# Down projection of a feed-forward: PSUM products copied by ScalarE and added to x by accumulating DMAs

## The chip, the cores and the metric

One core of one Trainium2 chip runs the program. The metric is the device time of one execution in microseconds (us); lower is better. A measurement of this kernel tells a change from none at about 2%.

## What is computed

Two sequences of 512 and 256 tokens, 1024 features wide, go through the same two-layer trunk in float32. Each layer is a half-weighted feed-forward, a mixer (layer 0: an S5 recurrence beside neighbourhood attention; layer 1: windowed attention), and a second half-weighted feed-forward. A norm ends the trunk.

```python
def swiglu(x, wg, wu, wd):
    return (jax.nn.silu(x @ wg) * (x @ wu)) @ wd        # wg, wu: 1024 x 2816, wd: 2816 x 1024
...
        x = x + 0.5 * swiglu(rms_norm(x, norm_ffn[layer, 0]), w_ffn_gate[layer, 0],
                             w_ffn_up[layer, 0], w_ffn_down[layer, 0])
```

The change concerns the last product of `swiglu`, the one with `wd`, and its addition to `x`.

## The kernel before

**Tiles.** The 768 tokens are six tiles of 128 tokens; `x` stays in SBUF as six tiles of 128 x 1024 float32, `x0` to `x5`, always visited in the order 4, 5, 0, 1, 2, 3. The program runs six stages one after the other: feed-forward 0, the mixer of the even layer, feed-forwards 1 and 2, the mixer of the odd layer, feed-forward 3.

**Arithmetic.** A float32 operand is used as two float32r parts, a rounded one and the rest: `split` (L88, L89) has ScalarE (ACT) write the rounded part and VectorE (DVE) the difference. Every product then takes three matmuls. Weights come through SyncE's DMA queue (SP) into `raw` tiles (seven buffers of 512 KB), are summed by DVE where the fast product needs it (L124 to L134), and are split into `whl` tiles (eight buffers). `take` keeps up to four split tiles ready ahead of the product that uses them.

**A feed-forward.** The 2816 features are 22 blocks, taken in 11 pairs, 0 to 10. For a pair, the gate and the up product (`quad`) are done by a Strassen-Winograd form with seven products of 12 matmuls each (L247): in order p1, p6, p5, p7, p2, p3, p4 from pair 2 on. They share PSUM banks: p1 is copied by ACT (L261); p6 goes to a second bank, from which DVE makes `u2` with that copy (L273); p5 to a third, copied by ACT (L279); p7 is then accumulated on top of p6's bank, so TensorE (PE) can start p7 only when L273 has read it. ACT applies silu (L314), DVE multiplies (L317), and the pair's activations are split into `hl`.

**The down projection.** `rows` has six steps, one for each token tile. A step makes two halves of 512 output features; a half is six matmuls into one of eight PSUM banks (L362). Then DVE computes `x = 0.5 * o + x` on that half straight from PSUM (L365). The steps of pair b-1 stand between the gate and the up product of pair b (`middle` in `ffn`). The steps of the last pair, 10, stand at the end with `tail` given: there, `before` and `after` start the next stage's norm on each tile.

**Order.** Within an engine instructions run in a fixed order, which a scheduler sets when the program is built; the order on PE and SP follows the source closely. GpSimd (POOL) has nothing to do in feed-forwards 1 to 3 but one small norm operation per tile. In feed-forward 0 it builds the matrices of S5 (`s5_matrices`), whose steps are spread between the steps of the pairs from pair 2 on (`next(extra, None)`). For each of 16 pairs of S5 groups, POOL computes two matrices (`start`, L579 to L595; the DMA W2d of L600 is queued in the middle of it), PE transposes one of them and makes small products (`finish`, L605 to L616), ACT copies the result, and POOL sends it out (`store`, DMAs W1d and Ed, L623 and L624). The next `start` reuses the space that W1d reads.

Of the kernel before, what the change touches and what calls it, by code (L numbers as in the profile page):

```python
# [37 lines left out]
# neighbourhood attention: (first query, queries, first key, keys) in the order (column, row)  # L38
NA_Q = [(0, 128, 0, 256), (128, 128, 64, 256), (256, 128, 192, 256), (384, 128, 256, 256),
        (512, 128, 512, 160), (640, 128, 608, 160)]  # L40
# key blocks (first key, keys) of the windows above
# [5 lines left out]
class Trunk:  # L47
# [20 lines left out]
    def warm(self, after):  # L68
        """have the table of the square root loaded as soon as the column "after" is there"""
        w = self.cp.tile([P, 1], F32, tag="warm", name="warm", bufs=2)  # L70
        self.nc.scalar.activation(w, after, AF.Sqrt, bias=self.one, scale=0.0)
# [13 lines left out]
    def split(self, hl, lo, src):  # L85
        """hl (rounded) + lo = src, exactly"""
        nc = self.nc
        nc.scalar.copy(hl, src)  # L88
        nc.vector.tensor_sub(lo, src, hl.bitcast(F32))  # L89

# [6 lines left out]
    def weights(self):  # L97
        """the weights of the whole trunk"""
# [15 lines left out]
        def quad(n, q, b, r1=None):  # L114
            """the parts and sums of two blocks of features; without the head if r1, the first, is given"""
            k = lambda z: (n, q, b, z)
            headed, r1 = r1 is not None, self.raw(self.a[n][q, 2 * b]) if r1 is None else r1
            a11, a12 = r1[:, :512], r1[:, 512:]
            if not headed:
                yield k("11"), self.part(a11)  # L120
            r2 = self.raw(self.a[n][q, 2 * b + 1])
            a21, a22 = r2[:, :512], r2[:, 512:]
            s1 = self.wp.tile([P, 512], F32, tag="st", name="st", bufs=2)
            v.tensor_add(s1, a21, a22)  # L124
            v.tensor_sub(a21, a11, a21)
            v.tensor_sub(a11, s1, a11)
            yield k("s2"), self.part(a11)
            yield k("s1"), self.part(s1)
            if b < 2:
                yield k("22"), self.part(a22)  # L130
            yield k("s3"), self.part(a21)
            if not headed:
                yield k("12"), self.part(a12)
            v.tensor_sub(a12, a12, a11)  # L134
            yield k("s4"), self.part(a12)
            if b > 1:
                yield k("22"), self.part(a22)
# [57 lines left out]
    def norm_half(self, t, out):  # L195
        """sum of squares of the first half of token tile t"""
        ss = self.cp.tile([P, 4], F32, tag="ss", name="ss", bufs=6)
        self.nc.scalar.activation(out[:, 0:512], self.x[t][:, 0:512], AF.Square, accum_out=ss[:, 0:1])  # L198
        self.nc.gpsimd.tensor_scalar(ss[:, 1:2], ss[:, 0:1], 1.0 / DM, EPS, ALU.mult, ALU.add)  # L199
        return ss  # L200

    def norm_rows(self, t, gb, out, ss, parts=1):
        """out = rms_norm of token tile t"""
        nc = self.nc
        nc.scalar.activation(out[:, 512:1024], self.x[t][:, 512:1024], AF.Square, accum_out=ss[:, 2:3])
        nc.scalar.activation(ss[:, 3:4], ss[:, 2:3], AF.Sqrt, bias=ss[:, 1:2], scale=1.0 / DM)
        nc.vector.reciprocal(ss[:, 0:1], ss[:, 3:4])
        for e in range(parts):
            c = slice(e * DM // parts, (e + 1) * DM // parts)
            nc.vector.scalar_tensor_tensor(out[:, c], self.x[t][:, c], ss[:, 0:1], gb[:, c], ALU.mult, ALU.mult)  # L210
# [7 lines left out]
    def gemm(self, o, w, act, k0, n, kk=range(KM), last=KM - 1):  # L218
        """o[128 features, n tokens] = w^T act, w stationary; w and act hold four blocks of 128 features to a tile"""
        for k in kk:  # L220
            for j, i in ((0, 0), (0, 1), (1, 0)):
                self.nc.tensor.matmul(o, w[k // 4][:, j, k % 4 * P : (k % 4 + 1) * P], act[i][k // 4][:, k % 4, k0 : k0 + n],  # L222
                                      start=k == 0 and (j, i) == (0, 0), stop=k == last and (j, i) == (1, 0))

    def ffn(self, q, norm, tail, extra=None):
        """gate and up by Winograd's form of Strassen's product over 2 blocks of features, of inputs and of tokens"""
# [4 lines left out]
        with ExitStack() as ctx:  # L231
# [18 lines left out]
            def quad(n, b, use):  # L250
                """steps of the four blocks; use(feature block, token half, value)"""
# [85 lines left out]
            for b in range(1, NF // 2):  # L337
                g, u = (z[2:] for z in (g1, u1)) if b == 1 else pair(b)
                middle = self.rows(hs, q, b - 1, pos)
                if b == NF // 2 - 1:  # L340
                    middle.insert(0, lambda: self.warm(at(1, 0)[:, 0:1]))
                for s in (*g, *middle, *u):
                    s()
                    if b > 1:
                        next(extra, None)
            for s in self.rows(hs, q, NF // 2 - 1, pos, tail):
                s()

    def rows(self, hs, q, b, pos, tail=None):
        """steps of x += 0.5 h wd over a pair of blocks of features"""  # L350
# [3 lines left out]
        def step(t):  # L354
# [3 lines left out]
            for half in range(2):  # L358
# [5 lines left out]
                xs = self.x[t][:, half * 512 : (half + 1) * 512]  # L364
                nc.vector.scalar_tensor_tensor(xs, o, 0.5, xs, ALU.mult, ALU.add)  # L365
                if tail and half == 0:
                    st["t"].before(t)
            if tail:
                st["t"].after(t)

        return [lambda t=t: step(t) for t in TILES]

    def out_pass(self, name, kb, half, act, tail=None):
        """steps of x[:, half] += act w over k-block kb (4 of 128 features); act(part, k) has all tokens"""
# [24 lines left out]
    def fgemm(self, f, hn, evac, norm=None, kk=KM):  # L399
        """steps of a feature block of act @ w, feature-major; f names the weights, evac(psum, first token, tokens)"""  # L400
# [17 lines left out]
    def s5_matrices(self, pool, spare):  # L418
# [10 lines left out]
        class Room:  # L429
            """carves blocks out of tiles"""  # L430
# [26 lines left out]
        def exp(out, x):  # L457
            """exp to float32's accuracy"""
# [51 lines left out]
        # (a - 1) / lambda  # L510
# [15 lines left out]
        # powers 0..8  # L526
# [40 lines left out]
        def start(q):  # L567
            """a pair of groups: W2 (state -> outputs), W1 (inputs -> state)"""
# [28 lines left out]
        def finish(q):  # L597
            """W1 transposed, E (inputs -> outputs)"""
# [44 lines left out]
    def mixer0(self, norm, tail):  # L643
# [4 lines left out]
        with ExitStack() as ctx:  # L648
            mp = ctx.enter_context(self.tc.tile_pool(name="mix0", bufs=1))

            # inputs of S5, in (chunk position, channel) rows
# [14 lines left out]
            def qkv(h):  # L666
                """steps of a head pair's values, queries and keys, in the order (column, row)"""
# [28 lines left out]
            def na(h):  # L696
                """steps of a head pair; q is overwritten by the output, feature-major"""
# [65 lines left out]
            # chunk inputs of the states; both directions run from slot to slot, the reversed one backwards in time  # L763
# [31 lines left out]
            # outputs of S5: chunk inputs through M, states before the chunk through W2  # L795
# [54 lines left out]
            # the neighbourhood half of the output projection around the gate of S5  # L850
# [25 lines left out]
    def mixer1(self, norm, tail):  # L876
        nc, a = self.nc, self.a
        hn = norm.hn
        with ExitStack() as ctx:
# [4 lines left out]
            # a key head's two parts above each other, the first part in the rows that its queries have  # L884
# [11 lines left out]
            # (query tile, first key tile, key tiles, first column of the bias)  # L896
# [20 lines left out]
            def att(m, store):  # L917
                """steps of the heads of key heads 2m and 2m+1"""
                bias, pend, pts, qq = [] if m else [bias0], {}, [], {}

                def queries(t):
                    """the first parts twice above each other, and the second parts"""
# [146 lines left out]
def weave(main, *sides):  # L1069
    """emit the steps of main with those of the sides spread between them"""  # L1070
    done = [0] * len(sides)
    for i, m in enumerate(main):
        m()
        for k, s in enumerate(sides):
            while done[k] < round((i + 1) * len(s) / len(main)):
                s[done[k]]()
                done[k] += 1
# [6 lines left out]
class NormOut:  # L1084
    """final rms_norm, a token tile at a time"""
# [17 lines left out]
class NormT:  # L1103
    """rms_norm, transposed to feature-major in two parts, a token tile at a time"""
# [41 lines left out]
class NormS(NormT):  # L1146
    """the same as the sums that ffn multiplies with; tokens of tiles 4, 5, 0 and of 1, 2, 3 face each other"""
# [46 lines left out]
    def rest(self):  # L1194
        """the parts that later products take, a step for each"""
# [39 lines left out]
def _na_index(t):  # L1235
    """row of the padded table for each (query, key) of query tile t"""
# [9 lines left out]
def _layout(i):  # L1246
# [13 lines left out]
    # heads of the odd layer: tile (m, r) holds head r of key heads 2m and 2m+1  # L1260
# [5 lines left out]
    # S5  # L1266
# [11 lines left out]
    # biases by constant index; the last entry of the padded table is the masked one  # L1278
# [26 lines left out]
```

## Time and profile before

| | us |
|---|---|
| median of 2 runs (2750.31 and 2751.83) | 2751.07 |
| span of the profiled execution | 2751.6 |
| PE busy in it | 2695.9 (98%) |
| DVE busy | 2008.4 (73%) |
| ACT busy | 1176.3 (43%) |
| POOL busy | 340.6 (12%) |
| share of PE in the chain that ended last | 92% |

The span is the time from the first to the last instruction of one profiled execution; the page gives no other time for that execution, and its span lies between the two runs. An engine's idle time costs only where another engine, in the end PE, waits for it. In the tables of stretches and in timelines, PEld is the loading of PE's weights, which runs beside its matmuls.

### The profile page before, as it was taken

Reading aid. Unit: us, or ns where it says so; the run is one execution under the profiler, and the core shown is the slowest. Engines: PE = TensorE matmul, PEld = TensorE weight load, DVE = VectorE, ACT = ScalarE, POOL = GpSimd, SP = SyncE. Lnnn points to the kernel's source line nnn. Section 1 sums busy time; section 2 is a strip of 40 time slices with the busy share of each in tenths; the row PEclk is TensorE's granted clock in tenths of the full one; section 3 lists DMA queues with packets and bytes.
Section 4 is the critical chain, followed back from the end, with each engine's and each line's share of the span. In section 5 each row is a group of like instructions: output and inputs, shape, how many; then the busy total and the mean of one; then the engine's idle time right before and its main releaser. Section 6 shows DMA issues by size and latency. Waiting matters only on the chain.

```text
span 2751.6 us, 38966 instructions
## 1 busy us (share of the span) xinstructions
PE 2695.9 (98%) x14636; PEld 2422.3 (88%) x14636; DVE 2008.4 (73%) x3878; ACT 1176.3 (43%) x2464; POOL 340.6 (12%) x688
## 2 busy tenths in 40 slices
PE   7999999998999999999999999999999999999998
PEld 7988988888888999999989999999876689999997
DVE  8967776772964887677789776767557678777776
ACT  6333333343565633333354333334457664333333
POOL 0156654300840000000000000000000000000000
PEclk9999999999999999999999999999999999999999
DMA  4122222316244222121203121211201123122221
GB/s 155 65 90 85 90 90 77 127 54 134 89 125 142 81 81 85 54 85 54 88 29 122 62 77 62 79 61 39 100 16 39 45 72 108 63 76 68 71 70 54
DMA packets 81245, 217.48 MB, mean 79 GB/s; under 512 B 22848, under 2 KB 29632, under 8 KB 80800
## 3 DMA queue, kind: packets, MB, share of 16 engines
q1 hardware_dynamic: 77152, 203.91, 23.4%
q0 software_dynamic: 3904, 11.08, 1.2%
q8 instruction: 115, 1.88, 0.3%
q14 instruction: 74, 0.61, 0.1%
HBM read 199.17 MB, written 17.89 MB: 79 GB/s over the span
## 4 chain that ended last, share of the span: by engine, by line
PE 92%; DVE 3%; DMA 2%; ACT 2%; POOL 1%; issue 1%; SPq 0%; DVEq 0%; ACTq 0%; POOLq 0%
PE ps L247 44%; PE ps L362 25%; PE ps L222 8%; PE ps L389 5%; PE ps L957 1%; PE ps L990 1%; PE ps L956 1%; PE ps L978 1%; PE ps L1133 1%; PE ps L1009 1%; PE ps L774 1%; PE ps L616 1%; DVE raw L210 1%; PE ps L746 1%; DVE whl L89 0%
## 5 line engine op out<-in xcount | busy, mean ns | idle before, releaser
L88 ACT CAST whl<-raw 128x512 fp32r<-128x512 f32 x796 | 480.3, 621 | 943.7 <-PE ps L362 446.6
L247 PE MATMUL ps<-bt,whl 128*128 128x384 f32 x4224 | 764.6, 336 | 8.9 <-DVE ct L273 8.9
L247 PEld LDWEIGHTS ps<-bt,whl 128*128 128x128 f32 x4224 | 737.9, 189 | 12.5 <-DVE ct L273 10.1
L362 PE MATMUL ps<-whl,hl 128*128 128x512 f32 x3168 | 732.7, 391 | 0.0
L89 DVE TENSOR_TENSOR whl<-raw,whl 128x512 fp32r<-128x512 f32 x796 | 550.6, 705 | 220.2 <-ACT whl L88 209.2
L362 PEld LDWEIGHTS ps<-whl,hl 128*128 128x128 f32 x3168 | 593.9, 188 | 123.5 <-ACT hl L88 0.9
L247 PE MATMUL ps<-b,whl 128*128 128x384 f32 x3168 | 580.3, 336 | 0.0
L247 PEld LDWEIGHTS ps<-b,whl 128*128 128x128 f32 x3168 | 555.1, 189 | 3.5 <-ACT hct L617 0.3
L365 DVE SCALAR_TENSOR_TENSOR x<-ps,x 128x512 f32<-128x512 f32 x528 | 361.5, 689 | 217.5 <-PE ps L362 215.3
L199 POOL TENSOR_SCALAR ss<-ss 128x1 f32<-128x1 f32 x42 | 11.3, 270 | 1787.2 <-ACT raw L198 1787.2
L222 PE MATMUL ps<-hn,whl 128*128 128x256 f32 (+1 forms) x1248 | 231.2, 342 | 1.4 <-ACT hn L88 1.4
L222 PEld LDWEIGHTS ps<-hn,whl 128*128 128x128 f32 x1248 | 191.8, 190 | 31.8 <-issue 3.3
L88 ACT CAST hl<-hct 128x384 fp32r<-128x384 f32 x176 | 86.9, 512 | 50.8 <-DVE hct L317 44.9
L389 PE MATMUL ps<-whl,ob 128*128 128x512 f32 x432 | 105.2, 399 | 0.0
L89 DVE TENSOR_TENSOR hl<-hct,hl 128x384 fp32r<-128x384 f32 x176 | 98.3, 577 | 7.7 <-ACT hl L88 7.4
L389 PEld LDWEIGHTS ps<-whl,ob 128*128 128x128 f32 x432 | 80.7, 190 | 19.7 <-issue 2.2
L279 ACT COPY ct<-ps 128x384 f32<-128x384 f32 x88 | 42.3, 481 | 102.4 <-PE ps L247 102.4
L314 ACT ACTIVATE hct<-ct 128x384 f32<-128x384 f32 x88 | 46.3, 526 | 91.3 <-DVE ct L285 79.9
L284 DVE TENSOR_TENSOR ct<-ps,hct 128x384 f32<-128x384 f32 x88 | 48.9, 556 | 29.3 <-PE ps L247 29.1
L124 DVE TENSOR_TENSOR st<-raw 128x512 f32<-128x512 f32 x88 | 62.6, 712 | 10.1 <-DMA raw<-in_w_gate 9.2
L958 DVE CUSTOM_DVE_ANT_0 raw<-ps,gb,sk 128x256 f32<-128x256 f32 (+1 forms) x96 | 48.6, 525 | 29.0 <-PE ps L957 25.8
L392 DVE TENSOR_TENSOR x<-ps,x 128x512 f32<-128x512 f32 x48 | 33.0, 688 | 48.6 <-PE ps L389 48.6
(235 smaller groups left out, 2632.8 us busy)
## 6 DMA issues: line engine op xcount, KB each, us to landing
raw<-in_w_gate SPq DMA_DIRECT2D x92, 512.0 KB, 3.6
raw<-in_w_up SPq DMA_DIRECT2D x92, 512.0 KB, 3.6
raw<-in_w_down SPq DMA_DIRECT2D x88, 512.0 KB, 3.7
raw<-in_w_in_even SPq DMA_DIRECT2D x16, 512.0 KB, 3.6
raw<-in_w_in_odd SPq DMA_DIRECT2D x10, 512.0 KB, 4.8
W2d<-raw POOLq DMA_DIRECT2D x16, 256.0 KB, 2.4
W1d<-hct POOLq DMA_DIRECT2D x16, 256.0 KB, 3.0
raw<-W1d SPq DMA_DIRECT2D x8, 512.0 KB, 5.5
```

The lines of the kernel that those rows point to most:

```text
L88: nc.scalar.copy(hl, src)
L89: nc.vector.tensor_sub(lo, src, hl.bitcast(F32))
L124: v.tensor_add(s1, a21, a22)
L222: self.nc.tensor.matmul(o, w[k // 4][:, j, k % 4 * P : (k % 4 + 1) * P], act[i][k // 4][:, k % 4, k0 : k0 + n], start=k == 0 and (j, i) == ...
L247: nc.tensor.matmul(o, w[:, j, k * P : (k + 1) * P], B[z][:, i, k], start=first and k == 0 and (j, i) == (0, 0), stop=k == 3 and (j, i) == ...
L279: nc.scalar.copy(bank["r5"], bank[3])
L284: v.tensor_add(u3, bank[2], bank["p1"])
L314: nc.scalar.activation(at(f, t), o, AF.Silu)
L362: nc.tensor.matmul(o, h[i][:, pos[t] * P : (pos[t] + 1) * P], w[half][:, j], start=n == 0 and (j, i) == (0, 0), stop=n == len(hs) - 1 and ...
L365: nc.vector.scalar_tensor_tensor(xs, o, 0.5, xs, ALU.mult, ALU.add)
L389: nc.tensor.matmul(o, act(i, k)[:, t * P : (t + 1) * P], st["w"][k][:, j], start=m == 0, stop=m == 11)
L958: nc.vector.tensor_tensor_reduce(p[:, e, :n], s[:, :n], bias[0][:, par * 4 + h, c0 : c0 + n], -1.0, sk[:, 1, hh + h : hh + h + 1], ALU.add ...
```

## The change

In all pairs but the last of a feed-forward, ACT multiplies the PSUM half by 0.5 into one half of a tile `y` (128 x 1024, three buffers), and after both halves POOL issues a DMA that adds the whole `y` tile to `x[t]` in SBUF. In the last pair, where `tail` is given, DVE's instruction stays. The program is also built with `dynamic_dma_scratch_size=4096`. Comments that the new file drops are left out here.

```diff
-                middle = self.rows(hs, q, b - 1, pos)
+                middle = self.rows(fp, hs, q, b - 1, pos)
...
-            for s in self.rows(hs, q, NF // 2 - 1, pos, tail):
+            for s in self.rows(fp, hs, q, NF // 2 - 1, pos, tail):
...
-    def rows(self, hs, q, b, pos, tail=None):
+    def rows(self, pool, hs, q, b, pos, tail=None):
...
-                xs = self.x[t][:, half * 512 : (half + 1) * 512]
-                nc.vector.scalar_tensor_tensor(xs, o, 0.5, xs, ALU.mult, ALU.add)
-                if tail and half == 0:
-                    st["t"].before(t)
+                if tail:
+                    xs = self.x[t][:, half * 512 : (half + 1) * 512]
+                    nc.vector.scalar_tensor_tensor(xs, o, 0.5, xs, ALU.mult, ALU.add)
+                    if half == 0:
+                        st["t"].before(t)
+                else:
+                    if half == 0:
+                        st["y"] = pool.tile([P, DM], F32, tag="y", name="y", bufs=3)
+                    nc.scalar.activation(st["y"][:, half * 512 : (half + 1) * 512], o, AF.Copy, scale=0.5)
             if tail:
                 st["t"].after(t)
+            else:
+                nc.gpsimd.dma_start(self.x[t], st["y"], accum_op=ALU.add)
...
-    nc = _bacc.Bacc("TRN2", target_bir_lowering=False, num_devices=1)
+    nc = _bacc.Bacc("TRN2", target_bir_lowering=False, num_devices=1, dynamic_dma_scratch_size=4096)
```

The order of instructions on PE and SP is the same before and after. Source lines above 349 have other numbers after: the new copy is L372, the accumulating DMA L376, and each line of `s5_matrices` is seven higher (L600 becomes L607, L623 becomes L630).

On ACT, in feed-forward 1 around the down projection of a pair, before: silu (L314), the casts of weights that follow it, and the copy of the up product's p1 (L261).

```order
L314 ACTIVATE hct<-ct 128x384
L88 CAST whl<-raw 128x512
L314 ACTIVATE hct<-hct 128x384
L88 CAST whl<-raw 128x512 x4
L261 COPY hct<-ps 128x384
L88 CAST whl<-raw 128x512
```

The same place after:

```order
L314 ACTIVATE hct<-hct 128x384
L372 ACTIVATE y<-ps 128x512 x10
L88 CAST whl<-raw 128x512
L372 ACTIVATE y<-ps 128x512
L88 CAST whl<-raw 128x512
L372 ACTIVATE y<-ps 128x512
L88 CAST whl<-raw 128x512 x2
L261 COPY hct<-ps 128x384
```

The twelve copies into `y` now stand between the last silu and the four casts, the last two of them among the casts; L261 stands behind all of them.

On POOL, in feed-forward 0 around the down projection of pair 3, before: the end of an S5 `start` and the `store` that follows.

```order
L600 DMA W2d<-raw 128x512
L592 TENSOR_TENSOR raw<-hct 128x2x128
L593 TENSOR_TENSOR hct<-s5k,raw 128x256
L594 TENSOR_TENSOR hct<-s5k,raw 128x256
L595 TENSOR_TENSOR raw<-hct 128x2x128
L623 DMA W1d<-hct 128x512
```

The same place after (x_81 and x_82 are token tiles 4 and 5, x_77 to x_80 tiles 0 to 3):

```order
L607 DMA W2d<-raw 128x512
L599 TENSOR_TENSOR raw<-hct 128x2x128
L600 TENSOR_TENSOR hct<-s5k,raw 128x256
L601 TENSOR_TENSOR hct<-s5k,raw 128x256
L602 TENSOR_TENSOR raw<-hct 128x2x128
L376 DMA x_81<-y 128x1024
L376 DMA x_82<-y 128x1024
L376 DMA x_77<-y 128x1024
L376 DMA x_78<-y 128x1024
L376 DMA x_79<-y 128x1024
L376 DMA x_80<-y 128x1024
L630 DMA W1d<-hct 128x512
```

All six accumulating DMAs of the pair stand behind the whole S5 `start`, and the `store` stands behind all six.

## Rows read from the trace of the kernel before

**Rows 1.** Stretches by stage: length, busy us (instructions) by engine, clock, DMA share, GB/s

```profile
core 0: us, PE busy (x) PEld busy (x) DVE busy (x) ACT busy (x) POOL busy (x), PEclk, DMA share, GB/s
25.00:600.00 575.00, 558.88 (x3116) 510.41 (x3116) 438.50 (x776) 210.75 (x427) 230.48 (x370) 0.98 0.26 86
926.00:1425.00 499.00, 499.00 (x2647) 468.06 (x2646) 387.55 (x649) 197.01 (x381) 0.91 (x4) 1.00 0.23 73
1433.00:1935.00 502.00, 502.00 (x2666) 470.52 (x2664) 389.90 (x653) 196.44 (x380) 1.76 (x4) 1.00 0.23 74
2241.00:2738.00 497.00, 497.00 (x2633) 466.15 (x2632) 383.85 (x643) 191.28 (x366) 0.84 (x3) 1.00 0.23 73
```

**Rows 2.** Chain that ended last, in feed-forward 1: start us, length us, what

```profile
1123.62 29.14 PE ps L247 x168
1152.77 16.36 PE ps L362 x72
```

**Rows 3.** Timeline, one down projection: start us, us, engine, instruction, [idle before <-releaser]

```profile
1152.61 16.52 PE L362 MATMUL ps<-whl,hl 128*128 128x512 f32 x72
...
1155.57 0.69 DVE L365 SCALAR_TENSOR_TENSOR x<-ps,x 128x512 f32<-128x512 f32 x1 [0.68 <-PE ps L362]
...
1167.12 0.62 ACT L88 CAST whl<-raw 128x512 fp32r<-128x512 f32 x1 [13.14 <-PE ps L362]
...
1171.07 6.40 PE L247 MATMUL ps<-bt,whl 128*128 128x384 f32 x36
...
1171.35 0.47 ACT L261 COPY hct<-ps 128x384 f32<-128x384 f32 x1
...
1173.42 0.56 DVE L273 TENSOR_TENSOR ct<-ps,hct 128x384 f32<-128x384 f32 x1 [0.36 <-PE ps L247]
```

**Rows 4.** Groups by line and shape: xcount | busy us, mean ns | idle before, releasers

```profile
L365 DVE SCALAR_TENSOR_TENSOR x<-ps,x 128x512 f32<-128x512 f32 x528 | 361.5, 689 | 217.5 <-PE ps L362 215.3
...
L124 DVE TENSOR_TENSOR st<-raw 128x512 f32<-128x512 f32 x88 | 62.6, 712 | 10.1 <-DMA raw<-in_w_gate 9.2 <-DMA raw<-in_w_up 0.9
...
L981 ACT COPY pt<-ps 128x512 f32<-128x512 f32 x56 | 30.1, 590 | 24.2 <-PE ps L978 23.9
...
L600 POOL DMA_DIRECT2D W2d<-raw x16 | 10.2, 634 | 0.0
```

**Rows 5.** DMA issues: count, KB each, median us from issue to landing

```profile
raw<-in_w_gate SPq DMA_DIRECT2D x92, 512.0 KB, 3.6
...
gb<-in_gqa_bias SPq DMA_DIRECT2D x2, 1536.0 KB, 6.8
```

**Rows 6.** Two stretches of feed-forward 1, columns as in rows 1

```profile
1123.62:1152.77 29.15, 29.15 (x170) 29.15 (x169) 24.23 (x42) 14.13 (x27) 0.00 (x0) 1.00 0.36 109
1152.77:1169.13 16.36, 16.36 (x73) 13.51 (x73) 9.52 (x15) 1.77 (x3) 0.00 (x0) 1.00 0.00 1
```

**Rows 7.** Waits of PE in 25 to 600 us: us in total, times, longest

```profile
PE ps L247 <- DVE ct L273: 8.9, 3, 4.0
...
PE ps L605 <- POOL raw L595: 5.7, 2, 2.9
```

**Rows 8.** Timeline of POOL and PE in feed-forward 0, columns as in rows 3

```profile
131.24 0.62 POOL L585 TENSOR_TENSOR hct<-s5k,raw 128x256 f32<-128x256 f32 x1
...
140.33 1.06 POOL L594 TENSOR_TENSOR hct<-s5k,raw 128x256 f32<-128x256 f32 x1
141.44 2.35 PE L247 MATMUL ps<-bt,whl 128*128 128x384 f32 x12 [1.93 <-DVE ct L273]
...
234.62 16.52 PE L362 MATMUL ps<-whl,hl 128*128 128x512 f32 x72
...
242.57 0.74 POOL L595 TENSOR_TENSOR raw<-hct 128x256 f32<-128x256 f32 x1
...
253.09 0.60 PE L605 MATMUL ps<-ident,raw 128*128 128x128 f32 x4
...
255.58 2.70 PE L247 MATMUL ps<-bt,whl 128*128 128x384 f32 x14
```

## The prediction

> **What bounds the kernel now.** I read the table of stretches first. In feed-forwards 1, 2 and 3 PE is busy for the whole of 499, 502 and 497 us, at a granted clock of 1.00, the 2.4 GHz level [rows 1]. The chain of waits says the same from the other side: in the steady part it consists of nothing but PE's products, 29.14 us of gate and up and 16.36 us of down projection for each pair, 45.5 us in all [rows 2]. DVE is the next engine, 388 of 499 us, and ACT has 197. So a busy DVE is not a waited-for DVE there. The one feed-forward in which PE idles is the first, 575.0 - 558.9 = 16.1 us [rows 1]. The waits of PE in it name DVE (8.9 us in three stops) and POOL (5.7 us in two) [rows 7]. That is all that a lighter DVE could give back in the stages that the change touches, about 0.5% of the run, before any cost.
>
> **What the change removes and adds.** Four stages x 10 pairs x 12 halves = 480 DVE instructions of 0.689 us go, 331 us of DVE. ACT gets 480 copies of 128x512 from PSUM; the nearest row is its copy of that shape, 0.590 us [rows 4], 283 us in all. POOL gets 240 accumulating DMAs of 512 KB. The PE order is unchanged, so in feed-forwards 1 to 3 removing DVE work gives 0: PE waits for nothing there.
>
> **ACT's copies** fall into a hole. Write R for the start of a down projection (1152.77). PE makes a half every 16.36 / 12 = 1.363 us. ACT idles for 13.14 us of that time, waiting for PE to free a weight buffer, until 1167.12 = R + 14.35 [rows 3]. Ten copies fit in front of that cast, one per half: the tenth half ends at R + 13.63, its copy at about R + 14.3. The other two stand among the casts. Price: 0, hidden by PE's own 16.36 us. Without that cover they would cost at most 12 x 0.59 = 7.1 us a pair.
>
> **The ring of three y tiles** is the wait that is added. DVE starts on the second half at 1155.57, R + 2.8 [rows 3]; ACT's copy in its place is done at R + 3.4, where the first DMA is issued, and the next two follow at R + 6.1 and R + 8.9. Tiles four, five and six reuse those buffers, and their first copies are due at R + 9.6, R + 12.3 and R + 15.0. Behind a waiting copy on ACT stand the casts and L261; DVE's L273 waits for L261, and PE's product p7 for L273. From the sixth tile's first copy to the end of L273 lie two copies (1.18), three casts (1.86), L261 (0.47) and L273 (0.56), with hand-overs 4.2 us. PE comes to p7 after three products, two of them in the 6.40 us row of three [rows 3]: R + 16.36 + 6.2 = R + 22.6. So PE stops only if the third DMA lands after R + 18.4.
>
> No accumulating DMA stands in this trace, so its time is an estimate. A load of 512 KB lands 3.6 us after its issue and one of 1536 KB after 6.8 [rows 5]: 2.0 us fixed and 1.6 us per 512 KB. Lower bound of the data time: one pass, 1.6 us. Upper: four passes, 6.4 us. I take two passes, y and x both read and the write beside them, 3.2 us, as the nearest to what must be moved. The DMA engines are idle in this stretch (share 0.00, against 0.36 in the products) [rows 6], so three transfers queue only behind one another: they land at R + 8.6, 11.8 and 15.0, each no later than its copy is due. Price 0. With data time s the third lands at R + 5.4 + 3s, which reaches R + 18.4 at s = 4.33 us. This is the figure from which the forecast tips. The smaller descriptor scratch could make an issue wait for an earlier DMA to land. At most three of these are in flight; I put 0, and as the other end one landing of 5.2 us, of which R + 18.4 - R - 15.0 = 3.4 us is slack: 1.8 us a pair.
>
> Here the Trainium skill (Collectives: The Full Stack, The bandwidth ceiling: the fold count and why AG ≠ RS ≠ AR) says that an add in the DMA path costs no cycles of its own but needs two source reads on one read ring, and so halves the rate of a copy. By it the data time would also be 3.2 us, worked out from the copy's row; no run here shows it yet.
>
> What else the transfers touch: the last three of a pair run into the products, beside weight loads at 109 GB/s [rows 6]. DVE's first use of a weight load waited for a DMA only 10.1 us in the whole run over 88 instructions [rows 4], so loads come early, and I price their delay at 0 (bounds 0 to 1.6 us a pair, one transfer). The last pair adds to x by DVE and needs pair 9's DMAs, which have the up product of pair 10 (14.6 us, half of 29.14) to land: 0.
>
> **Feed-forward 0, POOL.** Here POOL's order matters. In pair 3, W2d's group ends at 242.57 + 0.74 = 243.3, and all six DMAs stand behind it; the first y is ready at 234.8 + 3.4 = 238.2 [rows 8]. Issued back to back from 243.3, the third DMA lands at 243.3 + 2.0 + 9.6 = 254.9. PE stops after 234.8 + 18.4 = 253.2, or 255.7 since the small S5 products from 253.09 to 255.58 stand in front of p6 [rows 8]: between 0 and 1.7 us. In five more pairs some S5 instructions stand in front of a DMA, or the reverse. I take 2 us for all six, between 0 and 10. An issue itself takes POOL 0.63 us [rows 4], 60 x 0.63 = 38 us beside 230 of 575 busy: hidden.
>
> **Feed-forward 0, DVE.** The stop of 1.93 us at 141.44 comes while POOL works on its first S5 `start` beside DVE's sums [rows 8]. DVE's set-up for that start shares the two first down projections with 24 removed instructions, 16.5 us, so it should end some 10 us earlier and the start with it: I take 1.9 us back (bounds 0 and 1.9). The two other DVE stops come in the products, where nothing is removed but the last two halves: 0.
>
> The skill (SBUF — State Buffer, SBUF: two separate sides) adds that VectorE and GpSimd lock each other out of a shared port when a VectorE operation reads two SBUF tensors. L365 reads only one, so its removal would free no port. The trace agrees: POOL's sums take 0.62 us beside L365s and 1.06 us beside two-input sums [rows 8]. By that rule the later stops stay, which lowers the chance of the first rival below.
>
> **Sum.** 2751.6 (span) - 1.9 + 2 = 2751.7; the span lies 0.5 above the median of the runs. I predict 2751.
>
> **Rivals.**
> 1. The lighter DVE clears all stops of feed-forward 0: 2751 - 8.9 - 5.7 = 2736. For it: PE's waits name DVE. Against: two of the three stops lie in stretches that lose no DVE work.
> 2. POOL's single queue is the new wait, in feed-forward 0 alone: an S5 `start` held behind a DMA that waits for its y makes PE wait at L605, as it does twice already. At the upper price of 10 us: 2761, at twice that 2771.
> 3. The accumulating DMA is slow, and the ring of three holds ACT up: slower than before. It decides from s = 4.33 us. With both reads and the write in turn, s = 4.8, the third lands at R + 19.8, PE stops 1.4 us a pair, 40 pairs: 56 us, 2807. At four passes, s = 6.4: 6.2 us a pair, 2999. For it: no row shows this operation, and the slack is 3.4 us over three transfers. Against: the DMA engines are idle when it starts.
>
> That the change does not do what it says I leave without a chance: the built order shows copies and DMAs where the diff puts them.
>
> **How the numbers follow.** Forecast 0.60, rival 1 0.08, rival 2 0.15, rival 3 0.17. The forecast's own range is 2745 to 2757, from the bounds of its small terms. The whole range goes from 2738, near rival 1, to 2810, which takes in rival 3 up to three passes and leaves out its upper part. About 2% (55 us) is what a measurement tells from no change. Faster by more would need a PE that does less: 0.01. Slower by more is rival 3 from three passes on: 0.14. Within: 0.85.
>
> **What would show it.** Right: PE without idle time in feed-forwards 1 to 3; the accumulating DMA about 5 us from issue to landing; ACT near 1460 us busy, DVE near 1680; no wait of a y copy on a DMA above 1 us. Wrong: PE waits at L247 named L273, or ACT waits of L372 on the DMA, repeated at each pair (rival 3); PE waits at the transposes of S5 grown beyond 6 us (rival 2); a landing later than 6.2 us after the issue in feed-forwards 1 to 3 (R + 9.6 less R + 3.4) would make the ring step false.

## The result, and the profile after

The changed kernel takes 2774.49 us (2771.62 to 2777.36) against 2751.07: ratio 1.0082, interval 1.0062 to 1.0102. Run again later, in one batch with other variants, it took 2765.62 us, ratio 1.0062 (1.0040 to 1.0083). So it is 0.6 to 0.8% slower, where no change was predicted. That is less than the 2% at which a single measurement tells a change from none; both intervals lie wholly above 1. The time lies in the whole range that was given, 2738 to 2810, and above the forecast's own range of 2745 to 2757.

Stretches of the kernel after, columns as in [rows 1]; the rows are feed-forwards 0, 1, 2 and 3:

```profile
24.00:623.00 599.00, 572.25 (x3174) 521.54 (x3172) 375.19 (x670) 285.17 (x564) 285.58 (x431) 0.97 0.54 137
946.00:1447.00 501.00, 501.00 (x2658) 469.80 (x2657) 310.71 (x533) 268.61 (x505) 52.68 (x64) 1.00 0.56 136
1454.00:1951.00 497.00, 497.00 (x2634) 466.00 (x2633) 305.48 (x524) 263.37 (x492) 52.45 (x63) 1.00 0.56 136
2265.00:2770.00 505.00, 502.92 (x2656) 470.54 (x2655) 311.58 (x536) 265.70 (x503) 53.34 (x66) 1.00 0.56 137
```

Feed-forwards 1 and 2 are as full of PE work as before (the 2.1 idle us of the last row lie in its last 5 us, at the end of the stage). DVE gave up some 80 us in each, ACT took some 70, and the share of the DMA engines went from 0.23 to 0.56. The chain of waits there is the same as in [rows 2]:

```profile
1144.18 29.14 PE ps L247 x168
1173.32 16.36 PE ps L362 x72
```

The loss is in feed-forward 0, where 599.0 - 572.3 = 26.8 us are idle against 16.1 [rows 1]. To find the place I set the starts of the down projections beside each other. Timeline of PE in feed-forward 0, kernel before:

```profile
274.42 0.60 PE L605 MATMUL ps<-ident,raw 128*128 128x128 f32 x4
...
285.35 13.81 PE L362 MATMUL ps<-whl,hl 128*128 128x512 f32 x60
...
501.65 16.52 PE L362 MATMUL ps<-whl,hl 128*128 128x512 f32 x72
...
549.77 16.52 PE L362 MATMUL ps<-whl,hl 128*128 128x512 f32 x72
```

The same view of the kernel after, with the stops between them in brackets:

```profile
229.75 16.52 PE L362 MATMUL ps<-whl,hl 128*128 128x512 f32 x72
...
274.13 0.33 PE L612 MATMUL ps<-ident,raw 128*128 128x128 f32 x1 [3.83 <-POOL raw L599]
276.20 0.90 PE L612 MATMUL ps<-ident,raw 128*128 128x128 f32 x3 [1.74 <-POOL raw L602]
...
280.34 4.21 PE L247 MATMUL ps<-bt,whl 128*128 128x384 f32 x12
...
291.15 13.80 PE L362 MATMUL ps<-whl,hl 128*128 128x512 f32 x60
...
375.24 0.55 PE L612 MATMUL ps<-ident,raw 128*128 128x128 f32 x3 [1.19 <-POOL raw L602]
...
509.39 16.52 PE L362 MATMUL ps<-whl,hl 128*128 128x512 f32 x72
...
536.18 2.35 PE L247 MATMUL ps<-bt,whl 128*128 128x384 f32 x12 [1.38 <-DVE ct L273]
...
545.96 4.21 PE L247 MATMUL ps<-bt,whl 128*128 128x384 f32 x12 [3.27 <-DVE ct L284]
...
565.37 16.52 PE L362 MATMUL ps<-whl,hl 128*128 128x512 f32 x72
```

| from the start of | before, us | after, us | difference |
|---|---|---|---|
| the span to pair 3's down projection | 234.62 | 229.75 | -4.9 |
| pair 3's to pair 4's | 50.73 | 61.40 | +10.7 |
| pair 4's to pair 8's | 216.30 | 218.24 | +1.9 |
| pair 8's to pair 9's | 48.12 | 55.98 | +7.9 |

In sum +15.6, and the end of feed-forward 0 is late by as much. Two places lose, and each stop costs more than its idle time. From pair 3 to pair 4 PE stops 5.6 us in front of the S5 transposes; then 12 products take 4.21 us that take 2.35 elsewhere. After PE was busy for only 0.63 of 6 us, the clock has fallen to the 1.2 GHz level for 8 us (the second row's 0.50):

```profile
270.00:276.00 6.00, 0.63 (x3) 0.14 (x1) 3.28 (x5) 1.00 (x2) 5.74 (x8) 0.94 0.56 187
276.00:284.30 8.30, 8.10 (x39) 6.66 (x40) 1.52 (x3) 1.09 (x3) 3.63 (x11) 0.50 0.20 72
```

**The first place** is read on POOL's timeline of the kernel after:

```profile
239.33 2.67 POOL L376 DMA_DIRECT2D x<-y  x3
...
251.28 0.85 POOL L376 DMA_DIRECT2D x<-y  x1 [2.33 <-ACT y L372]
253.18 0.58 POOL L630 DMA_DIRECT2D W1d<-hct  x1 [1.05 <-ACT hct L625]
...
262.45 0.39 POOL L586 TENSOR_TENSOR hct<-s5k 128x32 f32<-128x32 f32 x1 [7.26 <-DMA W1d<-hct]
...
275.42 0.72 POOL L602 TENSOR_TENSOR raw<-hct 128x256 f32<-128x256 f32 x1
```

The six accumulating transfers of pair 3 leave between 239.3 and 252. Behind them W1d is issued at 253.18, and it lands after 9.1 us (the same one before took 4.2, and the median before was 3.0). The next S5 start writes into W1d's source tile, so POOL waits for it 7.26 us, finishes at 276.1, and PE stands at the transposes of 274. The same wait on POOL in the kernel before:

```profile
259.09 0.33 POOL L579 TENSOR_TENSOR hct<-s5k 128x32 f32<-128x32 f32 x1 [1.70 <-DMA W1d<-hct]
```

What differs is in the stretches of that time: the 16 DMA engines are full. First before, then after:

```profile
240.00:248.00 8.00, 8.00 (x37) 6.63 (x36) 4.15 (x6) 0.00 (x0) 3.14 (x5) 1.00 0.09 33
248.00:256.00 8.00, 8.00 (x56) 6.68 (x55) 6.00 (x10) 3.77 (x9) 1.13 (x2) 1.00 0.23 74
256.00:262.00 6.00, 6.00 (x37) 6.00 (x36) 2.64 (x4) 2.13 (x4) 3.91 (x10) 1.00 0.40 144
```

```profile
240.00:248.00 8.00, 8.00 (x39) 6.95 (x38) 0.00 (x0) 2.38 (x5) 2.85 (x4) 1.00 0.96 180
248.00:256.00 8.00, 7.72 (x58) 6.63 (x57) 5.95 (x10) 6.01 (x14) 3.70 (x6) 1.00 1.05 207
256.00:262.00 6.00, 6.00 (x37) 6.00 (x36) 4.75 (x9) 2.27 (x5) 0.00 (x0) 1.00 0.87 251
```

**The second place** is a weight load. In pair 8 a whole S5 start stands in front of the transfers again; the first three leave together at 519.3 to 522. The chain of waits of the kernel after:

```profile
520.52 9.48 DMA x<-y
...
532.98 9.94 DMA raw<-in_w_up
```

ACT and DVE at that time:

```profile
524.99 1.09 ACT L372 ACTIVATE y<-ps 128x512 f32<-128x512 f32 x2 [6.60 <-DMA x<-y]
...
542.94 0.69 DVE L124 TENSOR_TENSOR st<-raw 128x512 f32<-128x512 f32 x1 [6.81 <-DMA raw<-in_w_up]
```

ACT's seventh copy waits 6.60 us for a free y, with the weight casts queued behind it; DVE waits 18 us for a cast; so the buffer of the next load comes free late, the load leaves 23.6 us after the down projection's start instead of 19.2, meets full DMA engines and lands after 9.9 us (the same load before took 4.8). L124, and then L284, wait for it, and PE for L284. Here two things act together, the late buffer and the slow load, and no run parts them.

The rest of the first profile's 24 us arose in the mixers, which no part of the change touches: everything is 15.6 us late at their start and 20.5 us late at feed-forward 1, and 3.5 us more are lost in the odd mixer. Both times the granted clock is lower for 10 to 20 us: 0.52 from 845 to 855 in the first, where before shows 1.00; 0.78 and 0.88 from 2130 to 2150 in the second, where before shows 0.83 in one stretch of 10 us. The second run of the same kernel does not show that: its span of 2763.4 is late by 12.9 us at the end of feed-forward 0 and by 11.8 at the end.

### The profile page after: what moved, and what is told of

The parts are those of the page before. It is cut to its first block, busy times and chain, and to the rows that moved or that the text cites. A ratio compares the mean times of both kernels' runs of the same rounds, so it can differ in the third digit from the quotient of the medians.

```text
span 2775.6 us, 39523 instructions
## 1 busy us (share of the span) xinstructions
PE 2711.4 (98%) x14636; PEld 2434.1 (88%) x14636; DVE 1699.3 (61%) x3398; ACT 1452.5 (52%) x2944; POOL 549.8 (20%) x928
## 4 chain that ended last, share of the span: by engine, by line
PE 85%; POOL 5%; DMA 4%; issue 2%; DVE 2%; ACT 2%; SPq 0%; DVEq 0%; POOLq 0%; ACTq 0%
PE ps L247 40%; PE ps L362 22%; PE ps L222 8%; PE ps L396 5%; DMA W1d<-hct 2%; PE ps L964 1%; PE ps L997 1%; PE ps L963 1%; PE ps L985 1%; PE ps L1140 1%; DMA x<-y 1%; PE ps L1016 1%; PE ps L781 1%; DMA raw<-in_w_up 1%; PE ps L818 1%
## 5 line engine op out<-in xcount | busy, mean ns | idle before, releaser
L89 DVE TENSOR_TENSOR whl<-raw,whl 128x512 fp32r<-128x512 f32 x796 | 556.9, 710 | 710.7 <-ACT whl L88 697.9
L376 POOL DMA_DIRECT2D x<-y x240 | 208.9, 879 | 1431.7 <-ACT y L372 1198.6
L372 ACT ACTIVATE y<-ps 128x512 f32<-128x512 f32 x480 | 284.5, 598 | 291.8 <-PE ps L362 244.8
L314 ACT ACTIVATE hct<-ct 128x384 f32<-128x384 f32 x88 | 46.3, 526 | 91.6 <-DVE ct L285 78.9
L124 DVE TENSOR_TENSOR st<-raw 128x512 f32<-128x512 f32 x88 | 62.6, 712 | 31.8 <-DMA raw<-in_w_up 24.1
L88 ACT CAST whl<-st 128x512 fp32r<-128x512 f32 x88 | 54.1, 619 | 26.2 <-PE ps L247 26.2
L284 DVE TENSOR_TENSOR ct<-ps,hct 128x384 f32<-128x384 f32 x88 | 48.9, 555 | 30.4 <-PE ps L247 30.2
```

The source lines that it names most:

```text
L284: v.tensor_add(u3, bank[2], bank["p1"])
L314: nc.scalar.activation(at(f, t), o, AF.Silu)
L372: nc.scalar.activation(st["y"][:, half * 512 : (half + 1) * 512], o, AF.Copy, scale=0.5)
L376: nc.gpsimd.dma_start(self.x[t], st["y"], accum_op=ALU.add)
```

## The experiments

Theory Q put the cause in POOL's order and its one DMA queue. The later runs are about theory D: the DMA engines are full, and whatever waits for a landing is late. Each ratio is against the kernel before, run in the same batch. All of them lie under 2%, so what counts is the interval behind each, and the traces.

**Feed-forward 0 by DVE as before.**

```diff
-                if tail:
+                if tail or q == 0:
                     xs = self.x[t][:, half * 512 : (half + 1) * 512]
```

> Feed-forward 0 adds to x by DVE as before; feed-forwards 1 to 3 keep copies and accumulating DMAs, and the descriptor scratch stays at 4096. Theory Q (in feed-forward 0 the accumulating DMAs share POOL's program order and its one DMA queue with the S5 work, and hold it up): the loss is gone, 2751 within 4. Rival S (the smaller scratch, or 240 transfers as such, cost the time): the part of feed-forwards 1 to 3, 180 of 240 transfers, stays, so at least 2765.

2749.86 us, ratio 0.9998 (0.9987 to 1.0008). The loss is gone though 180 of 240 transfers and the small scratch are still there. Feed-forward 0 is the whole of it.

**Copy by ACT, addition by DVE.**

```diff
+            elif q == 0:
+                nc.vector.tensor_add(self.x[t], st["y"], self.x[t])
             else:
                 nc.gpsimd.dma_start(self.x[t], st["y"], accum_op=ALU.add)
```

> In feed-forward 0 ACT still copies to y, but DVE adds y to x; no accumulating DMA there. Theory Q: PE stops fall back to those of before, 2751 to 2757 (DVE now reads two SBUF tensors for 60 adds beside POOL). Rival A (the ACT copies themselves push back the weight casts): 2768 or more, since all 120 copies are still there.

2757.41 us, ratio 1.0023 (1.0013 to 1.0032), just above what was expected. With the copies alone, neither stop is there; so the ACT copies are not the cause of the two stops. PE's waits that remain are two of 5.1 us together at the S5 transposes, much like the two before, and five for L273, 12.7 us together (8.9 before); the additions (1.36 us each) load DVE more than what they replace, and POOL's sums are slower (L604, the last of a start, 1.20 us; 0.94 for its like before).

**An eighth of the bytes.**

```diff
+            elif q == 0:
+                nc.gpsimd.dma_start(self.x[t][:, 0:128], st["y"][:, 0:128], accum_op=ALU.add)
```

> In feed-forward 0 each accumulating DMA moves only 128 of 1024 columns (the other columns of x miss their addition); order, issues and the ring stay. Theory Q in its half 'data in the queue' (W1d lands 9.1 us after its issue because three 512 KB transfers are ahead of it): W1d lands within 4 us, no stop above 2 us at the S5 transposes of pair 4, ACT waits for y under 3 us; 2751 to 2758. Its other half, 'order of issue' (W1d is issued only after the last DMA has its y, the three first DMAs only after a whole start): the stops stay, 2766 to 2774.

2750.58 us, ratio 1.0003 (0.9993 to 1.0012). Same issues, same order, same ring: no loss. So it is the data, not POOL's order or the issues. The half of theory Q that put it on the order falls. Small transfers also free the y tiles sooner (ACT waits 1.7 us for one around pair 3, 7.9 in the changed kernel), so this run does not yet part a late W1d from a late y.

**W1d on ACT's queue.**

```diff
-            nc.gpsimd.dma_start(self.W1d[:, gs, :], w1e.rearrange("p (g n) -> p g n", g=2))
+            nc.scalar.dma_start(self.W1d[:, gs, :], w1e.rearrange("p (g n) -> p g n", g=2))
```

> W1d is issued by ACT on its own queue, not by POOL; all else as in the changed kernel. Theory Q: W1d leaves when its copy is there and has no 512 KB transfer ahead in its queue; it lands within 4 us, the stop of 5.6 us at 270 to 276 with its slow clock goes (about 10 us); the late weight load of pair 9 (ACT held by the ring behind a whole start) stays (about 7 us): 2760 to 2766. If the queue plays no part: 2774 within 4.

2769.16 us, ratio 1.0068 (1.0050 to 1.0086), between the two expected ranges and no better than the changed kernel's 1.0062. The queue was my suspect, and it is not it. Timeline of ACT, POOL and PE:

```profile
252.21 0.33 ACTq L630 DMA_DIRECT2D W1d<-hct  x1
...
262.34 0.24 POOL L586 TENSOR_TENSOR hct<-s5k 128x32 f32<-128x32 f32 x1 [8.03 <-DMA W1d<-hct]
...
274.26 0.33 PE L612 MATMUL ps<-ident,raw 128*128 128x128 f32 x1 [4.61 <-POOL raw L599]
```

W1d left 1 us earlier, on a queue with no other transfer of that time, and took 10.0 us (9.1 in the changed kernel). Beside engines that are already full, a queue of its own did not make it faster.

**The changed kernel again.**

> The changed kernel again, on one chip with the next three. 2771 to 2777; a lower value would mean that part of the first result was the clock in the mixers, where its profile shows a stretch at 0.52 that the kernel before did not have.

2765.62 us, ratio 1.0062 (1.0040 to 1.0083). Below the expected span, and its trace loses nothing in the mixers, so part of the first result was the mixers' clock; the stops at 274 (3.84 and 1.75 us) and for L284 (3.10) are the same.

**DVE in the two pairs only.**

```diff
-                if tail:
+                if tail or q == 0 and b in (3, 8):
```

> As the changed kernel, but in pairs 3 and 8 of feed-forward 0 DVE adds to x (12 of 60 transfers fewer). Theory D (the 16 DMA engines are full for some 20 us where a whole S5 start stands in front of the six transfers, and W1d or a weight load comes late there): the two drifts of 10.7 and 7.9 us go, 2752 to 2759. Rival (the cost is spread over all 60 transfers): a fifth of the loss goes, 2769 to 2773.

2758.19 us, ratio 1.0026 (1.0011 to 1.0041): about half of the loss goes with a fifth of the transfers. Both stops are gone, but a new one of 4.8 us stands at the S5 transposes of 321 to 324, after the down projection of pair 4. The places are not fixed; they move with the step at which an S5 pair meets a down projection.

**S5's start in five pieces.**

```diff
             gp.tensor_add(w2[:, :, 0], m1, m2)
+            yield
...
-                start(q)
-                for _ in range(8):
+                yield from start(q)
+                for _ in range(4):
```

> S5's start is given out in five pieces, a step apart, instead of at once; PE's order and all transfers stay. If the burst (three transfers held behind a whole start, six in a row after it) is what fills the DMA engines at the wrong time, the transfers of pair 3 leave earlier: 2755 to 2766. If only the bytes matter, wherever they stand: 2770 to 2777.

2768.20 us, ratio 1.0062 (1.0037 to 1.0087). (Four such `yield`s stand in `start`, after its groups of sums.) It settles nothing, since the order did not change where it should: the start before pair 3's transfers ran on POOL from 229.5 to 240.4, and the first three transfers still left together behind it. Whether an order exists in which the transfers meet nobody was not tried further.

**A copy instead of an addition.**

```diff
+            elif q == 0:
+                nc.gpsimd.dma_start(self.x[t], st["y"])
```

> In feed-forward 0 the transfer copies y over x instead of adding (the addition to x is left out there); same order, issues and bytes written. If the engine time of the addition counts (2.79 us of all 16 engines for 512 KB, against 1.66 for a load of the same size): landing near 3.8 us instead of 5.3, W1d within 6, 2751 to 2762. If the queue and its issues count, not the engines: 2770 to 2777.

2753.46 us, ratio 1.0008 (0.9996 to 1.0020). Stretches of pair 3:

```profile
240.00:248.00 8.00, 8.00 (x39) 6.91 (x38) 2.07 (x3) 4.84 (x9) 1.55 (x4) 1.00 0.82 325
248.00:256.00 8.00, 8.00 (x61) 7.23 (x60) 4.15 (x7) 3.93 (x10) 2.63 (x5) 1.00 0.77 246
256.00:262.00 6.00, 6.00 (x37) 6.00 (x36) 5.14 (x8) 2.58 (x6) 5.22 (x10) 1.00 0.01 3
```

Its DMA issues in feed-forward 0, count, size and median us to landing:

```profile
x<-y POOLq DMA_DIRECT2D x60, 512.0 KB, 3.1
```

The same bytes written in the same order, without reading x: the engines are free by 256, and W1d lands after 6.4 us at that place (9.1 in the changed kernel). The interval takes in 1, so nothing is left of the loss that can be told from none. So it is the engine time of the addition that tips it.

**A tile of its own for the sums of S5's start.**

```diff
-        m1, m2 = (w1e[:, e * 256 : (e + 1) * 256].rearrange("p (g t c) -> p g t c", g=2, t=CH) for e in range(2))
+        mm = pool.tile([P, 512], F32, name="s5m")
+        m1, m2 = (mm[:, e * 256 : (e + 1) * 256].rearrange("p (g t c) -> p g t c", g=2, t=CH) for e in range(2))
```

(`n1`, `n2` likewise; scratch 2048.)

> The changed kernel with a tile of their own for the sums of S5's start, which so far share theirs with W1d's source (room for it from a descriptor scratch of 2048); the start then needs no landed W1d. All transfers and PE's order stay. Theory D (the full DMA engines cost time where something waits for a landing): the stop of 5.6 us at the transposes of pair 4 goes with its slow clock, 10 us, and the stops near 167 and 448 shrink by some 3 us each; the late weight load of pair 9 stays: 2744 to 2758. If the S5 work is late because POOL is busy issuing and waiting for y, not for W1d: 2762 to 2768.

2755.26 us, ratio 1.0020 (1.0010 to 1.0029), 10 us below the changed kernel in another batch. All 60 accumulating transfers are there, W1d is no faster (4.7 us to landing in the median, 8.9 behind pair 3's transfers), and no stop at the S5 transposes is left. POOL behind pair 3's transfers, from W1d to the end of the next start, which now comes at 268.4, before PE reaches the transposes:

```profile
254.85 0.58 POOL L631 DMA_DIRECT2D W1d<-hct  x1 [0.98 <-ACT hct L626]
...
267.50 0.93 POOL L603 TENSOR_TENSOR raw<-s5m 128x256 f32<-128x256 f32 x1
```

From pair 3's to pair 4's down projection it takes 50.7 us, as in the kernel before, where the changed kernel takes 61.4. Waits of PE in 25 to 625 us:

```profile
PE ps L247 <- DVE ct L273: 18.2, 7, 4.0
...
PE ps L247 <- DVE ct L284: 1.1, 1, 1.1
```

For the first place, what had to go was the wait for the landing, not the transfers. The second place is not cured: the wait for the load of pair 9 stays, 5.8 us on DVE, PE's stop for L284 is 1.1 us, and the kernel stays 0.2% slower than before.

**The same tile in the kernel before.**

```diff
+        mm = pool.tile([P, 512], F32, name="s5m")
...
-    nc = _bacc.Bacc("TRN2", target_bir_lowering=False, num_devices=1)
+    nc = _bacc.Bacc("TRN2", target_bir_lowering=False, num_devices=1, dynamic_dma_scratch_size=4096)
```

> The kernel before with the same tile of its own (scratch 4096 makes room); no accumulating DMA. If the landing of W1d is what makes PE stop at 169 and 439: two stops of 2.9 us go, with the slow clock of about 4 us behind each, and the time falls to 2735 to 2743, below both kernels. If POOL's own work sets them: 2748 to 2752.

2748.54 us, ratio 0.9995 (0.9985 to 1.0005): missed. The two stops at the transposes went, as expected, and PE waits for DVE in their stead. Waits of PE in 25 to 625 us:

```profile
PE ps L247 <- DVE ct L273: 13.8, 6, 3.5
```

That was 8.9 us in three stops [rows 7]: the products that wait for DVE are next in line, a few us behind the transposes. This run is also the right partner of the previous one, from the same batch: with the tile in both kernels the change still costs 2755.26 - 2748.54 = 6.7 us, against 2765.62 - 2750.62 = 15.0 without it (2750.62 is the kernel before in the later batch of the changed kernel). So the wait for W1d, where the transfers made it longer, is about half of the loss. Of the rest, 3.0 us lie between pair 8's and pair 9's down projections (51.1 us against 48.1), and the other part was not traced to a cause. No version beat the kernel before by what can be measured.

## Why the prediction was wrong

- **Feed-forwards 1 to 3 at 0**: right, shown by the chain of 29.14 and 16.36 us and by the first experiment. Two of the named signs went against it all the same: in the first pair of each of these stages ACT waited 2.4 us for a y, and 13 of the 60 transfers of each landed later than 6.2 us, up to 9.8. PE did not stop for them; the slack before p7 covered them.
- **ACT's copies**: right in feed-forwards 1 to 3. They take 0.598 us (0.590 assumed), ten of them in front of the cast.
- **The transfer**: close. Median 5.3 us from issue to landing (5.2 estimated). Three that leave together free their y 2.6 us apart (ACT's copies at 244.10, 246.70 and 249.38 wait for them), so the data time is 2.6 us, not 3.2, far from the 4.33 at which rival 3 decides. An issue takes POOL 0.88 us, not 0.63; hidden, as the eighth of the bytes shows.
- **The rule on additions.** The Trainium skill (Collectives: The Full Stack, The bandwidth ceiling: the fold count and why AG ≠ RS ≠ AR) says, of the reduce step of a collective, that its add needs two source reads and so gets half the rate of a copy. The rates here agree: at a share of 1.05 of the engines the addition moves 197 GB/s (kernel with W1d on ACT's queue, 240 to 248), which is 188 at 1.00; over the same stretch the copy moves 325 GB/s at a share of 0.82, which is 396 at 1.00. That the second read is the reason no run shows by itself.
- **"I price their delay at 0 (bounds 0 to 1.6 us a pair, one transfer)"** is the first step that failed. It spread the transfers evenly. In pair 8 they are late by a whole start and lie in one row with the load: it lands 9.9 us after its issue, leaves 4.4 us late because ACT holds the casts, and PE loses 4.65 us in stops.
- **"In pair 3 ... between 0 and 1.7 us"** is the second, and the larger. I followed the transfers to p6 only, which did wait no more than that (a stop of 0.28 us at 255). I did not ask what else has to land behind them. W1d does, as the last of seven transfers in a row; the next S5 start waits for it, and PE 20 us later for that. The term of 2 us for all six pairs, between 0 and 10, came to 10.7 for this place alone, and to 7.9 more for pair 8 (10.9 and 5.1 in the second run). The trace of before had the row that bore on this, among POOL's waits in 25 to 600 us, but I priced POOL's queue alone:

```profile
POOL hct L579 <- DMA W1d<-hct: 19.0, 10, 3.4
```

- **The price of a stop**: I took idle time alone. The 5.85 us of stops from pair 3 to 4 cost 10.7, the 4.65 us from pair 8 to 9 cost 7.9; the difference is in the main the clock at its lower level.
- **The stop at 141 gone**: right (-1.9); pair 3's down projection starts 4.9 us earlier in all.
- **Rival 2** had the right stage, the right place (S5's transposes) and nearly the right price (10 us, twice that at the upper end), at a chance of 0.15. Its sign came too: PE's waits at the transposes grew from 6.3 to 13.4 us. Its mechanism was wrong where it cost most: the `start` behind pair 3 was held 7.26 us by W1d's landing, not by standing behind a DMA that waits for its y, and sending W1d 1 us earlier on another queue did not help.

## What to carry over

A transfer that is hidden for its own consumers still takes the DMA engines for its time (a share of 0.87 to 1.05 here over 22 us): ask for each one added which other landings fall into that stretch, and who waits for them; a queue of its own did not help the one that was late here. Look first for waits that only a shared buffer makes, since a tile of its own took away some 10 us that moving the transfer's queue did not. A long stop of PE costs more than its length, here another 3 to 5 us, most of it the slow clock behind it. When a cure works, give it to the kernel before as well: only that showed how much of the loss it had explained.

## What was not expected of the hardware

An accumulating transfer of 512 KB within SBUF took 2.6 us of all 16 engines by the spacing of its landings, 0.524 MB / 188 GB/s = 2.8 us by the rate; a copying one took 0.524 MB / 396 GB/s = 1.3 us. A store of 256 KB, 3.0 us to landing in the median before, took 9.1 us behind six of the former on the same queue and 10.0 us on another engine's queue. A descriptor scratch of 4096 showed no price: the kernel with DVE in feed-forward 0 runs at 2749.86 us with 180 accumulating transfers. What 2048 costs no run shows by itself, since the only kernel with it, at 2755.26 us, has the transfers of feed-forward 0 as well.
